# Two score blocks of a map in one accumulator bank, and the summing transfers of a value operand queued earlier

## Chip, cores and metric

One core of one Trainium2 chip. The metric is the device time of one execution in microseconds; the time of a kernel is the median of its timed runs.

## The reference

A decoder trunk of two layers on 512 tokens of width 1024, all in float32. Each layer is a token mixer and a gated feed-forward net, each followed by a residual sum and a layer norm.

```python
for i in range(2):
    h = multiscale_pool(x, ...) if i == 0 else diff_attention(x, ...)
    x = layernorm(ALPHA * x + h)
    x = layernorm(ALPHA * x + (silu(x @ w_gate[i]) * (x @ w_up[i])) @ w_down[i])
```

The change lies at the seam of layer 0's feed-forward net and layer 1's attention, and in the attention:

```python
q, k, v = split(x @ w_qkv, 3)          # 8 heads, 2 maps (c = 0, 1) of 64 columns each; v: 128 columns a head
for qb in range(4):                    # blocks of 128 queries
    s = q[c, block qb] @ k[c, : (qb + 1) * 128].T / 8       # causal: 128, 256, 384, 512 keys
    p = softmax(s + bias)              # bias by distance
    a = p[0] - lam * p[1]
    out = a @ v
```

## The kernel before, in words

**Precision.** A product of two float32 matrices is made as three products of parts: each operand is a rounded high part and the rest, a low part, and high x high, high x low and low x high are summed in an accumulator bank. ACT casts the high part, DVE subtracts it for the low part (`split`, L123 and L124).

**Banks.** There are eight accumulator banks of 128 x 512 float32. `bank(name)` (L62) takes the next one of a pool of eight; a product into it waits until the last reader of the name that had the bank earlier is done.

**Order.** The order on every engine is written out by hand: the code is the schedule, and each engine, and each queue of transfers, takes its instructions in program order. SP issues plain loads, POOL issues transfers that add into their destination ("accumulating" ones), and POOL also makes the small power operation of each layer norm (`spread_of`, L199).

**The end of layer 0's feed-forward net** (`ffn`). The down product is made by a seven-product scheme (Strassen's, in Winograd's form) in the order `DOWN = P1, Q5, P6, Q3, P7, P2, Q4`; each product runs over six pairs of rows of the hidden matrix (`PAIRS`). In the last one, Q4, the two output halves of the first 256 tokens are normed while the products run, and its last three pairs are run once per token block (`tail = 3`). After it the attention begins.

**The value product** of the attention uses the same seven-product scheme, `values(p, r, accs, w)` (L1078 for its products). Three of its weight operands are sums of rows of the weight array `wall`, and these sums are made by transfers:

- `tall`: rows `two_rows(0)`, loaded by SP, then `two_rows(1)` and `two_rows(2)` added by POOL (`tall_step`, L270 to L275). It is cut into parts `vt0`, `vt1` (`wide6`), the operand of product P6. Then `two_rows(3)` is added (L1298), cut into `vu0`, `vu1` (`wide4`), the operand of Q4.
- `short`, in a tile named `vals`: `two_rows(1)` loaded by SP, then `two_rows(2)` added by POOL (L1018, L1019); cut into `vs0`, `vs1` (`wide7`), the operand of P7.

P6, P7 and Q4 all gather in the two banks `va`; between them ACT copies `va` out. Head 0's query and key products stand between P2 and P6. Two further rows (`raw`, L113) are also completed by accumulating transfers on POOL, for the later product Q5.

**A head of the attention.** For head h the code issues, on TensorE: the query product (24 matrix products), for h > 1 a small product of head h - 2, the key product (24), ten transposes of head h - 1's map into three banks `at` (L1185), the scores of four query blocks, then head h - 1's value product `mix`. `scores(h, q)` takes two banks, one for each map c, and runs six products of 64 contraction rows: (query high, key high), (query low, key high), (query high, key low), each for c = 1 and c = 0, the two maps lying on rows 64 to 127 and 0 to 63. `softmax` (L1155 on DVE, L1160 on ACT) reads the banks. The three `at` banks are read by an ACT cast to `ah` and a DVE subtraction to `al`; a bank is free again after the second.

Of the kernel before, what the change touches and what calls it, by code (L numbers as in the profile page):

```python
# [18 lines left out]
P = 128  # L19
S = 512  # L20
# [7 lines left out]
HD = 64  # L28
# [26 lines left out]
def trunk(ctx, tc, x, wall, pscale, lam_p, subln, table, lng, lnb, band, first, onehot, out):  # L55
    nc = tc.nc
# [5 lines left out]
    def bank(name):  # L62
        return ps.tile([P, 512], F32, tag="bank", name=name)
# [206 lines left out]
    def tall_step(step):  # L270
        if step == 0:
            talls.append(keep.tile([P, 2, D], F32, tag="gb", name="tall"))
            nc.sync.dma_start(out=talls[0], in_=two_rows(0))
        else:
            nc.gpsimd.dma_start(out=talls[0], in_=two_rows(step), accum_op=ALU.add)  # L275
# [226 lines left out]
    def ffn(layer, late):  # L502
        n = 2 * layer + 1
        final = n == 2 * DEPTH - 1
# [3 lines left out]
        with tc.tile_pool(name=f"ffn{layer}", bufs=1) as fp:  # L508
# [58 lines left out]
            for k in range(HALF):  # L567
                j0 = index[k] = len(chunks)
                c = c0 + 4 * k
# [16 lines left out]
            for kind, j in steps:  # L586
                c, pair = chunks[j]
# [200 lines left out]
            accs = [(bank(f"g{layer}_{f}"), bank(f"u{layer}_{f}")) for f in range(early)]  # L788
# [104 lines left out]
            f = early  # L893
# [41 lines left out]
            done = store if final else None  # L935
            for p in DOWN:
                j0 = DOWN.index(p) * len(PAIRS)
                if p == "P2" and not final:
                    tall_step(0)
                if p in ("P1", "Q5", "P2"):  # L940
                    banks[p] = [bank(f"{p}_{layer}_{s}") for s in range(2)]
                accs = banks[{"P1": "P1", "Q5": "Q5", "Q3": "Q5", "P2": "P2"}.get(p, "P1")]
                together = len(PAIRS) - (tail if p == "Q4" else 0)
                for i in range(together):
                    j = j0 + i
                    prepare(j + 5, j + 4)
                    if p == "Q4":
                        if i == together - 1:
                            prepare(len(items), len(items))
                            ready(c1 + FB + 2)  # L950
                        for s in range(2):
                            if i == s:
                                spread_of(n, s)
                            if i == s + 1:
                                norm(n, s)
                    if (p, i) == ("Q4", 2) and not final:
                        tall_step(1)
                    multiply(j, accs, range(2))
                for s in range(2):
                    if p == "P1":  # L960
                        add_to(s, 0, accs[s], ALPHA)
                    elif p == "Q5":
                        add_to(2 + s, 1, accs[s], ALPHA)
                    elif p == "P6":
                        add_to(s, 1, accs[s], ALPHA, op=ALU.subtract)
                    elif p == "Q3":
                        add_to(s, 1, accs[s])
                        stat(n, s, 1)
                    elif p == "P7":
                        add_to(2 + s, 1, accs[s], op=ALU.subtract)  # L970
                        stat(n, 2 + s, 1)
                    elif p == "P2":
                        add_to(s, 0, accs[s])
                        stat(n, s, 0)
                    elif p == "Q4":
                        if s == 0 and not final:
                            turn(n, 0)
                        for i in range(len(PAIRS) - tail, len(PAIRS)):
                            if final and s == 0:
                                prepare(j0 + i + 5, j0 + i + 5)  # L980
                                if i == 1:
                                    spread_of(n, 0)
                                    spread_of(n, 1)
                                if i == 2:
                                    norm(n, 0, done)
                            multiply(j0 + i, accs, (s,))
                        add_to(2 + s, 0, accs[s], ALPHA)
                        stat(n, 2 + s, 0)
                        spread_of(n, 2 + s)
                        if final and s == 0:  # L990
                            norm(n, 1, done)
                        norm(n, 2 + s, done)
                        if not final:
                            if s == 0:
                                turn(n, 1)
                            ready(c1 + FB + 3 + s)
            if not final:
                tall_step(2)
            base[0] = c1 + FB


    def attention():
        n = 2
        with tc.tile_pool(name="attn", bufs=1) as ap:
            lp = ap.tile([P, 4, HD], F32, tag="bias", name="lp", bufs=2)
            nc.sync.dma_start(
                out=lp.rearrange("p a b -> p (a b)"),
# [125 lines left out]
                w1 = ap.tile([P, 4], F32, tag="w1", name=f"w1_{h}", bufs=2)  # L1133
                mid[h] = (mn, sm, w1)

            def scores(h, q):
                (qh, ql), (kh, kl) = qk[h, "q"], qk[h, "k"]
                wide = max((q + 1) * P, 256)
                accs = [bank(f"s{h}_{q}_{c}") for c in range(2)]
                qs = slice(q * P, (q + 1) * P)  # L1140
                for i, (a, b) in enumerate(((qh, kh), (ql, kh), (qh, kl))):
                    for c in (1, 0):
                        r = slice(c * HD, (c + 1) * HD)
                        nc.tensor.matmul(  # L1144
                            accs[c][:, :wide], a[r, qs], b[r, :wide], start=i == 0, stop=i == 2
                        )
                maps[h, q] = accs

            def softmax(h, q):
                mn, sm, _ = mid[h]  # L1150
                w = (q + 1) * P
                accs = maps.pop((h, q))
                for c in range(2):
                    p = soft[h][c][:, OFF[q] : OFF[q] + w]
                    nc.vector.tensor_tensor_reduce(  # L1155
                        out=p, in0=accs[c][:, :w], in1=biases[h][:, w - 1 :: -1] if w < S else biases[h][:, ::-1],
                        op0=ALU.add, op1=ALU.min, scale=1.0, scalar=3.0e38,
                        accum_out=mn[:, q, c : c + 1],
                    )
                    nc.scalar.activation(  # L1160
                        p, p, AF.Exp, bias=mn[:, q, c : c + 1], scale=-1.0,
                        accum_out=sm[:, q, c : c + 1],
                    )
# [107 lines left out]
            w = take(2)  # L1271
# [7 lines left out]
            w = take(2)  # L1279
# [55 lines left out]
            for h in range(HEADS):  # L1335
                if h > 0:
                    combine(h - 1, 3)
                if h > 0:
                    split_values(h - 1)
                if h == 0:  # L1340
                    scalars()
                if 1 < h <= SB + 1:
                    affine(n - 1, h - 2)
                if h == SB + 2:
                    load_gb(n)
                if h + 1 < HEADS:
                    load_bias(h + 1)
                if h > 0:
                    accs = [bank(f"{nm}{h}") for nm in "qk"]
                    w = take(2)  # L1350
                    ready(where[0] + {1: 3, last: 3}.get(h, 1))
                    query(accs[0], w[0])
                    split_query(h, "q", accs[0])
                    if h > 1:
                        root(h - 2)
                    query(accs[1], w[1])
                    ready(where[0] + {1: 4, last: 3}.get(h, 2))
                    if h > 1:
                        scaled(h - 2)
                    split_query(h, "k", accs[1])  # L1360
                    if h == 1:
                        w = take(2)
                        for r in range(2):
                            values("Q3", r, vc, w[r])
                        for s in range(2):
                            combined(part(0, 1, s), vc[s], part(0, 1, s), ALU.subtract)
                    transposed(h - 1)
                start_scores(h)
                for q in range(2):
                    scores(h, q)  # L1370
                    softmax(h, q)
                if h == 0:
                    for s in range(2):
                        combined(part(1, 1, s), vc[s], part(1, 1, s), ALU.subtract)
                for q in (2, 3):
                    scores(h, q)
                if h > 0:
                    mix(h - 1)
                if h == last:
                    ready(where[0] + 4)  # L1380
                for q in (2, 3):
                    combine(h, q - 2)
                    softmax(h, q)
                combine(h, 2)
# [144 lines left out]
```

## Time and profile before

| | us |
|---|---|
| median of 3 runs (lowest, highest) | 952.35 (951.37, 953.99) |
| the profiled execution's own time | 954.01 |
| its span, first to last instruction | 952.2 |
| TensorE busy | 933.8 (98%) |
| VectorE (DVE) busy | 788.1 (83%) |
| ScalarE (ACT) busy | 514.4 (54%) |
| GpSimd (POOL) busy | 126.5 (13%) |
| mean granted TensorE clock | 0.993 |

PE is TensorE's matrix products, PEld its weight loads. All positions are microseconds from the start of the span. In a row of the timeline stand the start, the duration, the engine, the line of the code, the operation, `output<-inputs`, the shapes and the number of instructions merged; in square brackets the idle time of the engine ahead of it and what ended it. Records of successive matrix products overlap, so the distance between two starts says what one costs, not its duration.

### The profile page before, as it was taken

Reading aid. Unit: us, or ns where it says so; the run is one execution under the profiler, and the core shown is the slowest. Engines: PE = TensorE matmul, PEld = TensorE weight load, DVE = VectorE, ACT = ScalarE, POOL = GpSimd, SP = SyncE. Lnnn points to the kernel's source line nnn. Section 1 sums busy time; section 2 is a strip of 40 time slices with the busy share of each in tenths; the row PEclk is TensorE's granted clock in tenths of the full one; section 3 lists DMA queues with packets and bytes.
Section 4 is the critical chain, followed back from the end, with each engine's and each line's share of the span. In section 5 each row is a group of like instructions: output and inputs, shape, how many; then the busy total and the mean of one; then the engine's idle time right before and its main releaser. Section 6 shows DMA issues by size and latency. Waiting matters only on the chain.

```text
span 952.2 us, 14942 instructions
## 1 busy us (share of the span) xinstructions
PE 933.8 (98%) x5712; PEld 832.4 (87%) x5712; DVE 788.1 (83%) x1158; ACT 514.4 (54%) x819; POOL 126.5 (13%) x152
## 2 busy tenths in 40 slices
PE   9999999999999999899999999999999999999996
PEld 8898899999988888688888878998899999988884
DVE  7859879999988778767888777779779999987778
ACT  6652444554564457466877853833344554564450
POOL 4121121110001102100211100211111110001101
PEclk9999999999999999999999999999999999999998
DMA  8287988986868977966576532396888886888942
GB/s 242 114 259 240 345 272 246 263 261 206 257 207 284 359 253 181 236 182 167 134 149 161 128 102 91 101 315 215 258 273 245 256 269 205 258 248 278 366 153 89
DMA packets 86039, 211.11 MB, mean 222 GB/s; under 512 B 15141, under 2 KB 26661, under 8 KB 85967
## 3 DMA queue, kind: packets, MB, share of 16 engines
q1 hardware_dynamic: 43420, 117.16, 37.4%
q0 software_dynamic: 18768, 58.20, 24.8%
q10 hardware_dynamic: 23778, 34.78, 10.2%
q8 instruction: 45, 0.74, 0.3%
q14 instruction: 28, 0.22, 0.1%
HBM read 173.40 MB, written 36.72 MB: 221 GB/s over the span
## 4 chain that ended last, share of the span: by engine, by line
PE 89%; DVE 5%; DMA 2%; ACT 2%; issue 1%; POOL 0%; DVEq 0%; SPq 0%; POOLq 0%; ACTq 0%
PE A L859 17%; PE P L926 14%; PE C L859 8%; PE Q L926 6%; PE B L859 4%; PE g L151 3%; PE u L151 3%; PE u L149 3%; PE u L150 3%; PE g L149 3%; PE g L150 3%; PE s L1144 2%; PE va L1078 2%; DMA tall<-in_wall 2%; PE q L149 1%; PE q L151 1%
## 5 line engine op out<-in xcount | busy, mean ns | idle before, releaser
L605 DVE TENSOR_TENSOR raw<-raw,raw 128x1024 f32<-128x1024 f32 x56 | 68.3, 1219 | 0.5
L123 ACT CAST xs<-hid 128x512 fp32r<-128x512 f32 (+1 forms) x60 | 34.7, 582 | 24.4 <-DVE hid L773 24.4
L124 DVE TENSOR_TENSOR xs<-hid,xs 128x512 fp32r<-128x512 f32 (+1 forms) x60 | 38.4, 642 | 7.8 <-ACT xs L123 7.8
L1160 ACT ACTIVATE p<-p,mn 128x128 f32<-128x128 f32 (+3 forms) x64 | 35.2, 552 | 16.0 <-DVE mn L1155 16.0
L249 ACT ACTIVATE y<-pt,bT,gT 128x128 f32<-128x128 f32 x80 | 30.0, 455 | 19.4 <-PE pt L235 19.4
L704 POOL DMA_DIRECT2D b<-in_wall x20 | 14.0, 705 | 174.6 <-DMA tsum<-b 82.2
L765 POOL DMA_DIRECT2D xs<-ssum x24 | 17.4, 725 | 141.5 <-PE Q L926 68.4
L199 POOL TENSOR_TENSOR rs<-rs,mhalf 128x1 f32<-128x1 f32 x16 | 12.6, 792 | 163.0 <-DVE rs L198 123.6
L637 DVE TENSOR_TENSOR hid<-sg,u 128x512 f32<-128x512 f32 x16 | 11.0, 686 | 27.2 <-PE u L151 16.5
L704 POOL DMA_DIRECT2D hid<-in_wall x24 | 18.7, 824 | 79.0 <-DMA tsum<-hid 41.3
L1155 DVE CUSTOM_DVE_ANT_0 p<-s,bias 128x128 f32<-128x128 f32 (+3 forms) x64 | 28.1, 485 | 0.7 <-PE s L1144 0.7
L741 ACT CAST v<-u 128x512 fp32r<-128x512 f32 x22 | 13.6, 620 | 27.3 <-DVE u L739 27.2
L124 DVE TENSOR_TENSOR xt<-y,xt 128x512 fp32r<-128x512 f32 x20 | 13.6, 690 | 13.5 <-ACT xt L123 13.4
L190 DVE BATCH_NORM_STATS2 st<-res 128x6 f32<-128x512 f32 x32 | 22.2, 695 | 1.1
L885 ACT ACTIVATE sg<-sg 128x512 f32<-128x512 f32 x14 | 8.9, 632 | 25.7 <-DVE sg L878 25.7
L705 POOL DMA_DIRECT2D hid<-in_wall x12 | 14.8, 1233 | 56.3 <-DMA hid<-in_wall 49.6
L653 ACT CAST xs<-hid 128x1024 fp32r<-128x1024 f32 x8 | 8.4, 1051 | 23.8 <-DVE hid L670 11.6
L1144 PE MATMUL s<-heads 64*128 64x256 f32 (+2 forms) x168 | 19.9, 353 | 0.0
L874 DVE TENSOR_TENSOR hid<-C,hid 128x512 f32<-128x512 f32 x14 | 9.7, 691 | 10.8 <-PE C L859 9.3
L1174 DVE SCALAR_TENSOR_TENSOR p<-p,sm,p 128x128 f32<-128x128 f32 (+3 forms) x32 | 17.7, 552 | 1.1
L870 ACT COPY hid<-C 128x512 f32<-128x512 f32 x14 | 8.2, 587 | 18.5 <-PE C L859 18.5
L124 POOL TENSOR_TENSOR sql<-sq,sqh 128x512 fp32r<-128x512 f32 x7 | 9.0, 1293 | 65.0 <-ACT sqh L123 65.0
(1187 smaller groups left out, 3678.1 us busy)
## 6 DMA issues: line engine op xcount, KB each, us to landing
raw<-in_wall SPq DMA_DIRECT2D x122, 512.0 KB, 4.9
r<-tsum SPq DMA_DIRECT2D x40, 512.0 KB, 4.5
hid<-in_wall POOLq DMA_DIRECT2D x36, 512.0 KB, 7.2
b<-in_wall POOLq DMA_DIRECT2D x30, 512.0 KB, 5.7
r<-in_wall SPq DMA_DIRECT2D x30, 512.0 KB, 4.7
tsum<-hid ACTq DMA_DIRECT2D x24, 512.0 KB, 6.0
ssum<-v ACTq DMA_DIRECT2D x22, 512.0 KB, 4.0
tsum<-b ACTq DMA_DIRECT2D x20, 512.0 KB, 4.9
```

The source lines that it names most:

```text
L123: nc.scalar.copy(dst_h, src)
L124: (low or nc.vector).tensor_tensor(dst_l, src, dst_h.bitcast(F32), op=ALU.subtract)
L149: nc.tensor.matmul(acc, ah, bh, start=start, stop=False)
L150: nc.tensor.matmul(acc, ah, bl, start=False, stop=False)
L151: nc.tensor.matmul(acc, al, bh, start=False, stop=stop)
L249: nc.scalar.activation(y[:, k, :], pt[:, k * P : (k + 1) * P], AF.Identity, bias=bT[:, n, kk : kk + 1], scale=gT[:, n, kk : kk + 1],)
L605: tt(t, raws[pair[0]], raws[pair[1]], op=ALU.add)
L704: nc.gpsimd.dma_start(out=t[:, j], in_=src[:, j])
L859: nc.tensor.matmul(o, w[:, c], x[:, kk, :], start=p in ("P1", "Q5", "P2") and f + kk + e == 0, stop=p in ("Q4", "Q3", "P2") and (f, kk, e) ...
L926: nc.tensor.matmul(accs[s], x[:, k, r], y[:, c], start=first and k == 0 and e == 0, stop=last and k == m - 1 and e == 2, skip_group_check= ...
L1144: nc.tensor.matmul(accs[c][:, :wide], a[r, qs], b[r, :wide], start=i == 0, stop=i == 2)
L1160: nc.scalar.activation(p, p, AF.Exp, bias=mn[:, q, c : c + 1], scale=-1.0, accum_out=sm[:, q, c : c + 1],)
```

## The change

Two edits.

1. The second and third transfer into `tall` are queued earlier: `two_rows(1)` at the start of Q4 in place of Q4's third pair, `two_rows(2)` at Q4's third pair in place of the end of the net. The first stays at the start of P2.
2. `scores` takes several query blocks. Blocks 0 and 1 are made by one call: for each map c one bank holds block 0 in columns 0 to 255 and block 1 in columns 256 to 511. The order of the twelve products is: both blocks' (query high, key high), both blocks' (query low, key high), both blocks' (query high, key low); within a block c = 0 comes ahead of c = 1, for blocks 2 and 3 too. A head takes six banks for its scores where it took eight.

```diff
             for p in DOWN:
                 j0 = DOWN.index(p) * len(PAIRS)
-                if p == "P2" and not final:
-                    tall_step(0)
+                if p in ("P2", "Q4") and not final:
+                    tall_step(0 if p == "P2" else 1)
...
                     if (p, i) == ("Q4", 2) and not final:
-                        tall_step(1)
+                        tall_step(2)
                     multiply(j, accs, range(2))
...
-            if not final:
-                tall_step(2)
             base[0] = c1 + FB
...
-            def scores(h, q):
+            def scores(h, *qs):
                 (qh, ql), (kh, kl) = qk[h, "q"], qk[h, "k"]
-                wide = max((q + 1) * P, 256)
-                accs = [bank(f"s{h}_{q}_{c}") for c in range(2)]
-                qs = slice(q * P, (q + 1) * P)
+                accs = [bank(f"s{h}_{qs[0]}_{c}") for c in range(2)]
+                outs = {}
+                for n, q in enumerate(qs):
+                    wide = max((q + 1) * P, 256)
+                    outs[q] = [acc[:, 256 * n : 256 * n + wide] for acc in accs]
                 for i, (a, b) in enumerate(((qh, kh), (ql, kh), (qh, kl))):
-                    for c in (1, 0):
-                        r = slice(c * HD, (c + 1) * HD)
-                        nc.tensor.matmul(
-                            accs[c][:, :wide], a[r, qs], b[r, :wide], start=i == 0, stop=i == 2
-                        )
-                maps[h, q] = accs
+                    for q in qs:
+                        for c in range(2):
+                            r = slice(c * HD, (c + 1) * HD)
+                            nc.tensor.matmul(
+                                outs[q][c], a[r, q * P : (q + 1) * P],
+                                b[r, : outs[q][c].shape[-1]],
+                                start=i == 0 and q == qs[0], stop=i == 2 and q == qs[-1],
+                                skip_group_check=True,
+                            )
+                for q in qs:
+                    maps[h, q] = [o[:, : (q + 1) * P] for o in outs[q]]
...
-                        out=p, in0=accs[c][:, :w], in1=...,
+                        out=p, in0=accs[c], in1=...,
...
                 start_scores(h)
+                scores(h, 0, 1)
                 for q in range(2):
-                    scores(h, q)
                     softmax(h, q)
```

More of the change, by code (lines that the diff above doesn't have):

```diff
@@ L1155, in softmax @@
                     nc.vector.tensor_tensor_reduce(
-                        out=p, in0=accs[c][:, :w], in1=biases[h][:, w - 1 :: -1] if w < S else biases[h][:, ::-1],
+                        out=p, in0=accs[c], in1=biases[h][:, w - 1 :: -1] if w < S else biases[h][:, ::-1],
                         op0=ALU.add, op1=ALU.min, scale=1.0, scalar=3.0e38,
```

## The prediction

> **What bounds the kernel now.** I read the page first, then the waits, the chain, the timelines of POOL, ACT and DVE around the seam, and the busy times by stretch.
>
> ```profile
> PE 933.8 (98%) x5712; PEld 832.4 (87%) x5712; DVE 788.1 (83%) x1158; ACT 514.4 (54%) x819; POOL 126.5 (13%) x152
> PE va L1078 <- DVE vals L1261: 4.1, 1, 4.1
> ```
>
> TensorE is busy for 98% of the span, so only its waits and its slow places are worth anything. The second row, the longest of TensorE's waits, lies where the change acts: product P6 of the value operand.
>
> ```profile
> 381.22 0.59 POOL raw L113
> 381.81 16.26 DMA tall<-in_wall
> 398.10 1.05 ACT vt0h L123
> ...
> 400.32 1.22 DVE vt1l L124
> 401.54 0.61 DVE vals L1261
> ...
> 402.29 0.77 PE L1078 MATMUL va<-vt0h,heads 128*128 128x512 f32 x1 [4.13 <-DVE vals L1261]
> 410.56 0.62 PE L1078 MATMUL va<-vs0h,heads 128*128 128x512 f32 x2
> 416.00 0.62 PE L1078 MATMUL va<-vu0h,xt 128*128 128x512 f32 x2
> 398.00:402.00 4.00, 0.15 (x1) 0.00 (x0) 2.82 (x3) 2.48 (x3) 0.16 (x1) 0.79 1.06 256
> 402.00:406.00 4.00, 3.71 (x9) 2.97 (x10) 2.02 (x4) 1.77 (x2) 1.02 (x1) 0.50 0.88 129
> 406.00:410.00 4.00, 4.00 (x17) 3.23 (x16) 3.40 (x4) 1.30 (x3) 0.00 (x0) 0.85 0.96 190
> ```
>
> The chain names the cause: the last addition into `tall` took 381.81 + 16.26 = 398.07 to land, then come the cast, the subtraction, the sum out of bank `va`, and only then P6. The wait costs 4.13 us, and more behind it: P6 runs from 402.29 to P7's start at 410.56, 8.27 us, while P7, the same 24 products, takes 416.00 - 410.56 = 5.44. The stretches say why: after the idle time the granted clock (third number from the end) is 0.50. That is 2.83 us more.
>
> The second place is the scores. Their line alone, by stretch, each from a head's first score product to the next product behind the scores (heads 0, 1 and 2, then the sum over all eight heads):
>
> ```profile
> 426.50:428.65 2.15, 2.13 (x24) 1.72 (x24) 1.00 0.82 200
> 446.29:448.93 2.64, 2.64 (x24) 1.96 (x24) 1.00 1.09 231
> 463.61:466.41 2.80, 2.80 (x24) 2.02 (x24) 1.00 0.95 171
> ...
> sum 21.58, PE 21.55 PEld 15.85; mean PE 2.69 PEld 1.98
> ```
>
> The same 24 products take 2.15 us in head 0 and 2.80 in head 2, at full clock, and TensorE counts as busy throughout, so no table of waits shows it. Head 2 on DVE and TensorE:
>
> ```profile
> 463.24 0.69 DVE L124 TENSOR_TENSOR heads<-k,heads 128x512 fp32r<-128x512 f32 x1 [0.93 <-ACT heads L123]
> 463.85 0.68 DVE L124 TENSOR_TENSOR al<-at,ah 128x512 fp32r<-128x512 f32 x1
> 464.45 0.68 DVE L124 TENSOR_TENSOR al<-at,ah 128x512 fp32r<-128x512 f32 x1
> 465.05 0.41 DVE L124 TENSOR_TENSOR al<-at,ah 128x256 fp32r<-128x256 f32 x1
> 465.38 0.28 DVE L1155 CUSTOM_DVE_ANT_0 p<-s,bias 128x128 f32<-128x128 f32 x1
> 463.61 0.39 PE L1144 MATMUL s<-heads 64*128 64x256 f32 x2
> 463.99 0.50 PE L1144 MATMUL s<-heads 64*128 64x256 f32 x4
> 465.19 0.83 PE L1144 MATMUL s<-heads 64*128 64x512 f32 x3
> 465.52 0.73 PE L1144 MATMUL s<-heads 64*128 64x512 f32 x4
> ```
>
> Two things meet. Block 0's third pair, which reads the keys' low part, starts at 463.99, right after DVE has made it (463.24 + 0.69 = 463.93). And block 3's first product starts at 465.19 alone and the next at 465.52: just after the second and the third `al` subtraction end (465.13 and 465.46). These read the transposes' banks `at`. I infer that block 3's two banks, and one of block 2's (the first `al` ends at 464.53), are those of `at`, so the scores wait for DVE to empty them, and the two maps' products fall out of step.
>
> **Edit 1, the transfers.** No byte is added; two issues move.
>
> ```profile
> 338.64 0.38 SPq L273 DMA_DIRECT2D tall<-in_wall  x1
> DMA to landing us min/median/max: 8.4/12.8/16.3
> 361.62 0.95 POOL L199 TENSOR_TENSOR rs<-rs,mhalf 128x1 f32<-128x1 f32 x1 [37.87 <-DVE rs L198]
> 364.48 1.23 POOL L275 DMA_DIRECT2D tall<-in_wall  x1
> 391.54 1.19 POOL L1019 DMA_DIRECT2D vals<-in_wall  x1 [7.97 <-DMA vals<-in_wall]
> 401.84 1.18 POOL L1298 DMA_DIRECT2D tall<-in_wall  x1 [9.10 <-DVE vt1l L124]
> ```
>
> The first addition now waits on POOL only for the load issued at 338.64. Even at the slowest landing of `tall`'s three additions, 16.3, that load is in by 355, ahead of Q4's first power operation at 361.62, for which POOL has waited 37.87 us, so the POOL work behind it is not held. Issued by 355, it lands by 355 + 12.8 = 368 at the median and at 347 + 12.8 = 360 if the load takes 8.4. The second addition now stands behind Q4's two power operations, where the first one was: 364.48, or 368 if the first is late. It lands at 377 (+12.8), at the latest at 368 + 16.3 = 384. It is no longer behind the `raw` addition of 381.22. What the first addition collides with are SP's loads for Q4's last pairs. Bounded by the spread of landings above, these come 16.3 - 8.4 = 7.9 us later. The cover is that the code prepares four pairs ahead of the products (`prepare(j + 5, j + 4)`); a pair is 12 products, half of P7's 24, so 2.7 us, and four are 10.9. I take 0; without the cover it would be up to 7.9.
>
> What is late next?
>
> ```profile
> 392.92 1.06 ACT L1294 COPY vals<-vb 128x512 f32<-128x512 f32 x2
> 404.23 1.05 ACT L123 CAST vs0h<-vals 128x1024 fp32r<-128x1024 f32 x1 [3.65 <-DMA vals<-in_wall]
> 412.69 1.05 ACT L123 CAST vu0h<-tall 128x1024 fp32r<-128x1024 f32 x1
> ```
>
> - P6: ACT reaches the cast of `vt0` behind the copies, at 392.92 + 1.06 = 393.98 instead of 398.10. P6 starts 402.29 - 398.10 = 4.19 later, at 398.17. TensorE is free at 402.29 - 4.13 = 398.16. The whole wait goes, and with it the half clock.
> - P7 would start at 398.17 + 5.44 = 403.6. `short` must be in by 401.3 (cast and subtraction, 1.05 + 1.23). Now it lands at 404.23; its issue at 391.54 stood behind `tall`'s transfer in POOL's queue until 398.07, so its own bytes took 6.2. Without that: 391.54 + 1.2 + 6.2 = 399; unchanged: 404.2. I take 399.
> - Q4 would start at 409.0. The last addition to `tall` is issued when `vt1` is made, at 401.84 - 4.1 = 397.7; it is behind `short` again, and now ends at 401.84 + 8.4 = 410.2, 6.0 after it. So 399 + 6 = 405 against a need of 409.05 + 0.23 - 2.3 = 407. Unchanged, 410.2, it is 3.3 late.
>
> So edit 1 gives 4.13 + 2.83 = 6.96 us; bounds 6.96 - 3.3 - 2.83 (a second idle stretch at half clock) = 0.8 and 6.96.
>
> By the Trainium skill, "TensorE: Matmul & The Clock Gate", section "What's actually happening", an idle window of about 3.4 us puts the array on half clock. The trace agrees: 4.13 us idle, granted 0.50. By that rule a rest of 3.3 us would be at the edge of paying again.
>
> **Edit 2, the scores.** No product is added or taken away. The low keys' first use moves from the third pair to the fifth. Head 0 and the start of head 2's block 2:
>
> ```profile
> 427.22 0.28 PE L1144 MATMUL s<-krso,qsqh 64*128 64x256 f32 x2
> 427.34 0.34 PE L1144 MATMUL s<-ksq,qsqh 64*128 64x384 f32 x1
> ...
> 464.57 0.50 PE L1144 MATMUL s<-heads 64*128 64x384 f32 x3
> 441.79 0.69 DVE L124 TENSOR_TENSOR heads<-k,heads 128x512 fp32r<-128x512 f32 x1 [1.67 <-ACT heads L123]
> ```
>
> A pair of the two maps' products costs 427.34 - 427.22 = 0.12 there. The low keys are now needed four pairs, at least 0.48, after the first product; they come 0.32 after it (463.93 - 463.61). That wait goes. Two banks fewer a head shift the rotation by two names: blocks 2 and 3 take the banks of older readers, at most one of `at`, emptied at 464.53, 0.92 after the start, when block 3 begins at 6 x 0.12 + 3 x 0.18 = 1.26 (a pair's 0.12, by its width). So I expect every head at head 0's 2.15: 21.58 - 8 x 2.15 = 4.38 us. Bounds: nothing, 0, and 4.38.
>
> What may become late: block 0's softmax must now wait for the whole shared bank, 12 products instead of 6. In head 2 DVE comes to it at 465.38, 1.77 after the first product; the twelve are done after about 0.72 + 0.28 = 1.0, so free. In head 0 DVE does wait, about 0.5 longer, and has 1.67 idle later, at 441.79. A head's period shrinks by 0.65 for DVE:
>
> ```profile
> 498.16 0.69 DVE L124 TENSOR_TENSOR heads<-k,heads 128x512 fp32r<-128x512 f32 x1 [0.85 <-ACT heads L123]
> ```
>
> DVE waits 0.85 a head for the keys, more than 0.65, so it still keeps up; only just.
>
> A page speaks of just such banks: the Trainium skill, "PSUM — Partial Sum Buffer", section "PSUM bank collisions raise a hardware error", says that products of two different row tiles may not write one bank at the same time. Here each shared bank belongs to one map, one row half, so by that rule nothing new collides; no run here shows it yet.
>
> **Sum.** 6.96 + 4.38 = 11.34. Against the profiled execution's 954.01: 942.7; against the median of the runs, 952.35: 941.0. TensorE is bound from there to the end, and the later loads are tied to buffers that it frees, so nothing gives it back.
>
> **The rivals.**
> - *DVE becomes the bound in the heads.* For: 0.85 idle is little above 0.65, and head 0's softmax starts later. Against: DVE's idle time is TensorE's doing. Then edit 2 gives between 0 and 4.38: 941.0 to 945.4.
> - *The next transfer is late.* `vu` lands as late as now: 3.3 lost, 944.3; with half clock again, 947.1. For: POOL's queue is full there. Against: one megabyte less in it.
> - *Slower: the shared bank takes the maps' products out of step.* Place: the 12 products a head of blocks 0 and 1. Now they take 0.96 in head 2 (463.61 to 464.57), 0.08 each. If each waited for the product ahead to be done, 0.28 (the row at 427.22), a head loses 12 x 0.20 = 2.4, eight heads 19.2: 941.0 + 19.2 = 960.2. It decides from 11.34 / 96 = 0.12 us a product on. Against: each bank has one writer at a time, and the net's banks A, B and C hold two column halves in the same way, of which the list of waits names none.
> - *Nothing happens*: POOL is held by something else, and the banks are not the cause: 952.35.
>
> **How the numbers follow.** Forecast 0.72; DVE 0.10; late transfer 0.10; out of step 0.05; nothing 0.03. The runs of this kernel spread over 0.28%, so 0.3% (2.9 us) is about what a measurement can tell from no change. Faster by more: 0.72 + 0.10 + 0.10 = 0.92; within: 0.03; slower: 0.05. The forecast's own range is 941.0 with 1.7 either way (1.3, half the runs' spread, and 0.05 a head for reading the stretches); with the DVE case it holds 0.82: 939.3 to 945.4.
>
> **What would show it.** Right: no wait of `va` on L1261, P6 taking 5.44, the clock at 1.00 there; the additions to `tall` issued near 347 and 364; scores at 2.15 in every head. Wrong: a new wait of `va` at `vs0h` or `vu0h`; DVE without idle time ahead of `heads<-k` and TensorE waiting on it at `at` or `s`; scores longer than 2.8.

## The result and the profile after

| | before | after |
|---|---|---|
| median of 4 runs each (lowest, highest), us | 952.75 (951.37, 953.99) | 942.77 (942.32, 943.55) |
| profiled execution's own time | 954.01 | 942.9 |
| its span | 952.2 | 941.1 |
| mean granted TensorE clock | 0.993 | 0.997 |

The ratio is 0.9897, 95% interval 0.9879 to 0.9914: 10.0 us less. The forecast was 941.0, range 939.3 to 945.4, 92% for faster.

The page and the list of TensorE's waits of the changed kernel, the rows that answer to the first two of the prediction:

```profile
PE 926.7 (98%) x5712; PEld 828.5 (88%) x5712; DVE 786.9 (84%) x1158; ACT 514.2 (55%) x819; POOL 126.7 (13%) x152
PE va L1076 <- DVE vals L1266: 0.2, 1, 0.2
```

The share of TensorE is 98% as before. The wait of 4.1 us is down to 0.2. The seam on TensorE (first the last product of head 0's key, then the first products of P6, P7 and Q4), and the clock in the stretches behind it:

```profile
397.34 0.39 PE L151 MATMUL k<-xt,w73l 128*128 128x512 f32 x1
397.94 0.47 PE L1076 MATMUL va<-vt0h,heads 128*128 128x512 f32 x1 [0.21 <-DVE vals L1266]
403.50 0.39 PE L1076 MATMUL va<-vs0h,heads 128*128 128x512 f32 x1
408.94 0.39 PE L1076 MATMUL va<-vu0h,xt 128*128 128x512 f32 x1
398.00:402.00 4.00, 4.00 (x18) 3.29 (x19) 2.35 (x4) 2.44 (x3) 0.68 (x1) 1.00 0.79 112
402.00:406.00 4.00, 4.00 (x20) 3.30 (x18) 3.47 (x4) 2.92 (x5) 0.00 (x0) 1.00 0.86 170
```

P6 starts 0.60 after the last key product, of which 0.23 is that product itself, and takes 5.56 us; the clock stays at 1.00 where it was 0.50. POOL and ACT of the changed kernel show why:

```profile
344.97 1.23 POOL L275 DMA_DIRECT2D tall<-in_wall  x1 [21.62 <-DMA r<-tsum]
361.21 0.95 POOL L199 TENSOR_TENSOR rs<-rs,mhalf 128x1 f32<-128x1 f32 x1 [15.02 <-DVE rs L198]
364.07 1.21 POOL L275 DMA_DIRECT2D tall<-in_wall  x1
390.49 1.21 POOL L1017 DMA_DIRECT2D vals<-in_wall  x1 [8.69 <-DMA vals<-in_wall]
397.49 1.19 POOL L1303 DMA_DIRECT2D tall<-in_wall  x1 [5.79 <-DVE vt1l L124]
393.74 1.06 ACT L123 CAST vt0h<-tall 128x1024 fp32r<-128x1024 f32 x1
399.56 1.05 ACT L123 CAST vs0h<-vals 128x1024 fp32r<-128x1024 f32 x1 [3.31 <-DMA vals<-in_wall]
406.08 1.05 ACT L123 CAST vu0h<-tall 128x1024 fp32r<-128x1024 f32 x1
```

The two additions go out at 345 and 364. (The first row names `r<-tsum` as what ended POOL's wait; by the transfers' landings it was as forecast the load of `tall`, whose last part landed at 344.39, while that `r` was in only at 345.64.) The cast of `vt0` at 393.74 waits for no transfer any more, `short` is in at 399.56 instead of 404.23, and `vu0` is cast at 406.08 without a wait. The scores' line by head (heads 0, 1, 2, and the sum over eight):

```profile
419.92:422.05 2.13, 2.13 (x24) 1.71 (x24) 1.00 0.89 197
439.70:441.84 2.14, 2.13 (x24) 1.74 (x24) 1.00 1.06 241
456.51:458.65 2.14, 2.14 (x24) 1.74 (x24) 1.00 0.83 155
...
sum 17.09, PE 17.07 PEld 13.86; mean PE 2.13 PEld 1.73
```

Every head takes what head 0 took: 17.09 in all where it was 21.58. In head 2 block 3's first products no longer follow the third subtraction out of the `at` banks:

```profile
457.95 0.41 DVE L124 TENSOR_TENSOR al<-at,ah 128x256 fp32r<-128x256 f32 x1
458.09 0.63 PE L1145 MATMUL s<-heads 64*128 64x512 f32 x4
```

Block 3's products start, in pairs, at 458.09, while that subtraction runs until 457.95 + 0.41 = 458.36; in the kernel before, the second of them started 0.06 after its end.

**Where the span's 11.1 us came from**, by places on TensorE: 0.4 lies ahead of the change (SP's issue of `tall` at 338.2 for 338.64) and isn't its work; from there to Q5's first product 6.2, which is the whole difference of the seam, so the loads that the earlier addition might have delayed cost nothing that shows there; to head 7's transposes 3.8 (heads 1 to 6); from there to the end 0.7 (head 7).

### The profile page after: what moved, and what is told of

The parts are those of the page before. It is cut to its first block, busy times and chain, and to the rows that moved or that the text cites. A ratio compares the mean times of both kernels' runs of the same rounds, so it can differ in the third digit from the quotient of the medians.

```text
span 941.1 us, 14941 instructions
## 1 busy us (share of the span) xinstructions
PE 926.7 (98%) x5712; PEld 828.5 (88%) x5712; DVE 786.9 (84%) x1158; ACT 514.2 (55%) x819; POOL 126.7 (13%) x152
## 4 chain that ended last, share of the span: by engine, by line
PE 89%; DVE 6%; ACT 3%; issue 1%; POOL 0%; DVEq 0%; ACTq 0%; POOLq 0%
PE A L859 17%; PE P L926 14%; PE C L859 9%; PE Q L926 6%; PE B L859 4%; PE g L151 3%; PE u L151 3%; PE u L149 3%; PE u L150 3%; PE g L149 3%; PE g L150 3%; PE s L1145 2%; PE va L1076 2%; PE q L149 1%; PE q L151 1%; PE k L149 1%
## 5 line engine op out<-in xcount | busy, mean ns | idle before, releaser
L704 POOL DMA_DIRECT2D b<-in_wall x20 | 14.0, 706 | 173.6 <-DMA tsum<-b 49.6
L705 POOL DMA_DIRECT2D b<-in_wall x10 | 12.3, 1230 | 38.1 <-DMA b<-in_wall 38.1
```

Source lines behind the costliest of these rows:

```text
L704: nc.gpsimd.dma_start(out=t[:, j], in_=src[:, j])
```

## The experiments

The theory: the seam gains because the second addition no longer stands in POOL's queue behind the additions to `raw`; the scores gain because blocks 2 and 3 no longer wait for the banks of the transposes, and, a smaller and separate thing, because the low keys are needed later. The rivals are in the expectations. The table has the time, the sum of the scores' stretches over eight heads, and the seam: TensorE's idle time ahead of P6, P6's duration, and the way from the last key product's start to Q5's first product. The kernel before was run beside each group, and took 952.72 to 954.16; where that matters, a time is given both against the changed kernel's median and by how far each is under the kernel before beside it.

| kernel | median us | kernel before beside it | scores, sum | idle | P6 | seam |
|---|---|---|---|---|---|---|
| before | 952.75 | | 21.6 | 4.30 | 7.82 | 23.23 |
| after | 942.77 | 952.75 | 17.1 | 0.37 | 5.56 | 17.04 |
| transfers only | 946.25 | 952.72 | 21.6 | 0.00 | 5.53 | 16.64 |
| scores only | 949.20 | 952.72 | 17.1 | 5.24 | 7.11 | 23.46 |
| shared, block by block | 943.04 | 952.72 | 17.9 | 0.06 | 5.54 | 16.71 |
| own banks, high first | 946.60 | 952.72 | 21.8 | 0.00 | 5.54 | 16.65 |
| wait filled | 951.10 | 954.16 | 21.6 | 0.34 | 5.56 | 17.01 |
| first early, second late | 947.65 | 954.16 | 17.1 | 4.14 | 7.18 | 22.43 |
| both at third pair | 949.55 | 954.16 | 17.1 | 0.00 | 5.44 | 16.55 |
| after, again | 942.71 | 953.33 | 17.1 | 0.01 | 5.56 | 16.68 |
| sum ahead of cut | 942.18 | 953.33 | 17.1 | 0.00 | 5.44 | 16.63 |
| map order back | 942.46 | 953.33 | 17.0 | 0.00 | 5.54 | 16.65 |
| second ahead of raw | 944.67 | 953.60 | 17.1 | 0.27 | 6.79 | 18.58 |

(In "wait filled" the last key product comes 4 us later because of the added ones, so its seam is no gain by itself. P6 is taken from its first product to P7's first; in "second ahead of raw" its 6.79 holds a wait of P7.)

### Edit 1 alone, edit 2 alone

```diff
+                if p in ("P2", "Q4") and not final:
+                    tall_step(0 if p == "P2" else 1)   # and step 2 at Q4's third pair; scores as before
```

> Edit 1 alone: the two additions into tall are queued earlier, the scores are as before. If the seam is worth what the two traces show there (from the last key product's start to Q5's first product 23.23 us before, 17.04 after), this kernel is 6.2 us under the kernel before, about 946.6, with P6 starting within 0.6 us of the last key product at full clock and the scores still at 2.64 to 2.80 a head. Rival: the gain needs both edits (head 0's earlier start only lets the scores wait longer); then it is under 6 us and the scores lengthen.

Measured: 946.25, 6.5 us under the kernel before (ratio 0.9933, 0.9920 to 0.9947). The scores stay at 21.6. The transfers give their 6.2 to 6.6 us by themselves (the two seams, 23.23 - 17.04 and 23.23 - 16.64); the rival falls.

```diff
+                scores(h, 0, 1)    # and the new scores(); tall_step(1), tall_step(2) where they were
```

> Edit 2 alone: blocks 0 and 1 share banks, the additions into tall are as before. If the scores' gain is their own (8 x 2.70 before, 8 x 2.14 after: 4.49 us), this kernel is 4.5 us under the kernel before, about 948.3, with 2.14 a head and the wait of P6 unchanged near 4.3 with the clock at half behind it. Rival: DVE's slack is used up, so that part comes back as waits at the transposes or the key split; then it is under 3.5 us.

Measured: 949.20, 3.5 us under (0.9959, 0.9947 to 0.9972, that is 2.7 to 5.0 us). Its trace has the whole gain of the scores, 17.1, and the wait ahead of P6, in this execution longer than before:

```profile
PE va L1078 <- DVE vals L1268: 5.1, 1, 5.1
```

The interval holds the expected 4.5 and the rival's "under 3.5" alike, so the medians do not decide; the traces do. From Q5's first product to the end of the span the kernel before takes 952.2 - 421.0 = 531.2 us and this one 947.2 - 420.7 = 526.5: 4.7 less, as in the changed kernel (941.1 - 414.4 = 526.7). So nothing of the scores' gain came back behind them, and the rival falls. The two edits alone add up to 6.5 + 3.5 = 10.0, the gain of both; that it agrees to a tenth is chance, as each has an interval of more than 1 us either way.

### Order and sharing, apart

```diff
-                for i, (a, b) in enumerate(((qh, kh), (ql, kh), (qh, kl))):
-                    for q in qs:
+                for q in qs:
+                    for i, (a, b) in enumerate(((qh, kh), (ql, kh), (qh, kl))):
```

> The changed kernel with only the order of the twelve products put back: block 0's three pairs, then block 1's, still in shared banks. If the wait for the low keys and the bank waits are two separate things, only the wait for the low keys returns: 0.16 us in heads 2 to 7, about 1 us over the changed kernel, scores at 2.30. Rival one: the order is what made the gain; then the scores are at 2.6 to 2.8 and the kernel is 3.5 to 4.5 us over the changed one. Rival two: only the banks count: no difference.

The scores by head (heads 0, 1, 2, sum):

```profile
419.74:421.87 2.13, 2.13 (x24) 1.72 (x24) 1.00 0.92 161
439.53:441.67 2.14, 2.14 (x24) 1.74 (x24) 1.00 1.06 228
456.34:458.61 2.27, 2.27 (x24) 1.78 (x24) 1.00 1.07 199
...
sum 17.94, PE 17.93 PEld 14.12; mean PE 2.24 PEld 1.77
```

Sharing alone, with the old order, keeps most of the gain: 0.13 to 0.17 a head comes back in heads 2 to 7, and nothing in head 1, where another product stands between the key's cut and the scores. That is 0.85 us in the trace, as the theory had it. The median, 943.04, is 0.3 over the changed kernel, too little to be told by times (its runs reach from 942.65 to 943.36).

```diff
-                accs = [bank(f"s{h}_{qs[0]}_{c}") for c in range(2)]
-                    outs[q] = [acc[:, 256 * n : 256 * n + wide] for acc in accs]
+                    outs[q] = [bank(f"s{h}_{q}_{c}")[:, :wide] for c in range(2)]
...
-                                start=i == 0 and q == qs[0], stop=i == 2 and q == qs[-1],
+                                start=i == 0, stop=i == 2,
```

> The changed kernel with only the sharing put back: four banks for blocks 0 and 1, but the new order, high parts of the keys first. If blocks 2 and 3 wait for the banks of the transposes, whose last subtraction ends 1.85 us after the first score product, that end pins the scores whatever is won ahead of it: 2.64 in head 1 and 2.80 in heads 2 to 7 as before, 4.4 us over the changed kernel. The order alone would then be worth nothing. Rival: the order is worth its 0.16 a head, scores at 2.64; then it is 3.5 over the changed kernel.

```profile
419.16:421.50 2.34, 2.34 (x24) 1.87 (x24) 1.00 0.73 151
439.14:441.77 2.63, 2.63 (x24) 1.95 (x24) 1.00 1.06 223
456.45:459.25 2.80, 2.80 (x24) 2.02 (x24) 1.00 0.98 192
...
sum 21.75, PE 21.74 PEld 15.91; mean PE 2.72 PEld 1.99
```

With a bank of their own for each block, the new order is worth nothing: 2.80 in heads 2 to 7 as in the kernel before, 946.60, 3.8 us over the changed kernel. What is won at the low keys is waited for at the banks, whose release is tied to DVE's last subtraction. So the bank is the cause and the order is worth something only once the bank wait is gone. In head 2 block 3's first two products start at 458.03 and 458.36, each 0.06 after the end of one of DVE's last two subtractions out of `at`, as in the kernel before. (Head 0, which has no transposes ahead of it, takes 0.21 longer here than in any other kernel. There block 3's second product starts at 420.61, 0.06 after DVE's second read of block 0 has ended, 420.26 + 0.29 = 420.55. In the new order block 0 is done, and so read, later, and I infer that block 3 takes its banks: the same wait for another reader.)

### The clock behind the wait

```diff
+            for k in range(6):            # 18 of the key's 24 products, once more
+                mm3(wide(accs[1], 0, S), tuple(t[:, k * P : (k + 1) * P] for t in w[1]), x_at(k, 0, S), k == 0, k == 5)
             query(accs[1], w[1])
```

> The kernel before, with TensorE kept busy in its wait ahead of P6: the first 18 of the 24 products of head 0's key are run twice (18 x 0.227 = 4.1 us of the 4.3 that it idles). Nothing else changes. If the slow P6 (7.82 us where P7 takes 5.44) comes from the clock that falls in the idle time, P6 runs at clock 1.00 in 5.44 and the kernel is 2.4 us under the one before, about 950.3, though it does more work. Rival: P6 is slow because its operands arrive slowly; then P6 stays near 7.8 and the time at 952.7.

P6's and P7's first products, and the stretch of P6:

```profile
402.50 0.47 PE L1078 MATMUL va<-vt0h,heads 128*128 128x512 f32 x1 [0.18 <-DVE vals L1261]
408.06 0.39 PE L1078 MATMUL va<-vs0h,heads 128*128 128x512 f32 x1
402.00:406.00 4.00, 3.82 (x17) 2.93 (x16) 2.09 (x4) 1.62 (x2) 1.18 (x1) 1.00 0.81 129
```

P6 starts when it did, at 402.5, but at clock 1.00, and takes 5.56 for 7.82. The kernel does 4.1 us more work and is 3.1 us faster (0.9970, 0.9959 to 0.9982, that is 1.7 to 3.9 us); the two traces account for about 2 of it: P6 is shorter by 2.26 and starts 0.21 later. The slow P6 was the clock, not its operands.

### Where the second addition stands in POOL's queue

```diff
-                    if (p, i) == ("Q4", 2) and not final:
-                        tall_step(2)                      # back to the end of the net; step 1 stays early
```

> The changed kernel with only the second addition put back to the end of the net. If what counts is that this addition stands in POOL's queue behind the addition to raw at 380.7, it is issued at about 381 and lands at 395 to 398 again: the wait of P6 and the half clock are back, 4 to 6.2 us over the changed kernel, 947 to 949. Rival: the first addition's earlier landing frees the transfer engines, the second lands by 393 and the kernel stays at 943.

```profile
380.66 1.55 POOL L275 DMA_DIRECT2D tall<-in_wall  x1
401.02 0.47 PE L1076 MATMUL va<-vt0h,heads 128*128 128x512 f32 x1 [3.99 <-DVE vals L1266]
408.20 0.39 PE L1076 MATMUL va<-vs0h,heads 128*128 128x512 f32 x1
400.00:404.00 4.00, 2.98 (x8) 2.41 (x9) 3.20 (x5) 2.21 (x3) 1.18 (x1) 0.69 0.43 51
```

The addition goes out at 380.66 as in the kernel before, the wait is back with the half clock behind it (0.69 is the mean of that stretch: the clock fell to 0.50 at 401.51, when P6 had just begun), and the time is 947.65. That is 4.9 over the changed kernel's median, and 6.5 under the kernel before beside it where the changed kernel was 10.0 under, so 3.5 over by that reckoning; the seam is 22.43 - 17.04 = 5.4 longer. With the first addition early and the second late the idle time is 4.14; the two traces with both late have 4.30 and 5.24. So the early first addition alone hardly moves this wait.

```diff
-                if p in ("P2", "Q4") and not final:
-                    tall_step(0 if p == "P2" else 1)
+                if p == "P2" and not final:
+                    tall_step(0)
...
                     if (p, i) == ("Q4", 2) and not final:
+                        tall_step(1)
                         tall_step(2)
```

> The changed kernel with the first addition left at Q4's third pair, as in the kernel before, and the second right behind it. The second must wait on POOL until the first has landed (364.1 + about 12 = 376), and the power operation of the next token block, which POOL did at 372.5, stands behind it. If POOL's order is a real price, that operation comes near 378, the norm and the transposes behind it 5 us late, TensorE idles about 5 us there and pays half clock once: 5 to 8 us over the changed kernel, 948 to 951, while P6 itself no longer waits for tall. Rival: the power operation has slack; then the kernel is within 1 us of the changed one and the early start of the first addition was not needed.

POOL, the wait that appears, and the clock behind it:

```profile
377.12 1.20 POOL L275 DMA_DIRECT2D tall<-in_wall  x1 [11.77 <-DMA tall<-in_wall]
377.89 1.02 POOL L199 TENSOR_TENSOR rs<-rs,mhalf 128x1 f32<-128x1 f32 x1
PE pt L235 <- DVE res L208: 6.0, 1, 6.0
376.00:380.00 4.00, 0.18 (x1) 0.18 (x2) 1.05 (x2) 0.10 (x1) 2.77 (x3) 0.88 0.27 30
380.00:384.00 4.00, 4.00 (x14) 3.52 (x15) 3.76 (x7) 2.99 (x8) 0.00 (x0) 0.50 1.03 202
```

The second addition waits on POOL for the first to land; the norm's power operation behind it comes at 377.89, TensorE idles 6.0 us at the transposes that need that norm and then runs at 0.50. 949.55 is 6.8 over the changed kernel's median; against the kernel before beside it, it is 4.6 under in place of 10.0, so 5.4 over. P6 waits for nothing. So both moves belong together: the first makes room for the second to be issued without holding POOL.

```diff
-                    if (p, i) == ("Q4", 2) and not final:
-                        tall_step(2)
...
                             if s == 0:
                                 turn(n, 1)
+                            else:
+                                tall_step(2)              # ahead of the second addition to raw
                             ready(c1 + FB + 3 + s)
```

> The changed kernel with the second addition put between Q4's last power operation and the second addition to raw: POOL reaches it at about 379, some 15 us later than in the changed kernel and 2 us earlier than in the kernel before. With a landing of 12.8 to 16.3 us it is in at 392 to 395, and P6 would wait between nothing and 1.5 us, too short for the clock to fall if the fall needs the 4 us that it had in the other traces: 0 to 1.5 us over the changed kernel, P6 in 5.5. Rival: any wait drops the clock; then P6 takes about 7 and the kernel is 2 to 3 us over the changed one.

```profile
401.25 1.05 ACT L123 CAST vs0h<-vals 128x1024 fp32r<-128x1024 f32 x1 [5.48 <-DMA vals<-in_wall]
PE va L1076 <- ACT vals L1313: 1.1, 1, 1.1
402.00:406.00 4.00, 2.93 (x14) 2.09 (x13) 3.66 (x4) 3.65 (x6) 0.00 (x0) 1.00 0.77 153
```

`tall` is in, at 393.26, by the time that ACT comes to its cast (393.29, without a wait), and P6 idles only 0.27, as in the changed kernel (0.37) for DVE's sum out of `va`. But now `short` is late: it is cast at 401.25, ACT's copy of `va` stands behind its casts, and P7 waits 1.1 us for that copy. The time, 944.67, is 1.9 over the changed kernel's median, or 8.9 under the kernel before beside it in place of 10.0, so 1.1 over; the seam is 1.5 longer. The size is near what was expected, but it comes by another wait. The clock stays at 1.00 through this wait: the rival that any wait drops it falls.

### Two small variations

> The changed kernel once more, as the measure for the two beside it: 942.8, 9.9 us under the kernel before.

> The changed kernel with DVE's sum out of the banks va (which P6 overwrites) put ahead of the cut of vt0 and vt1. In the changed kernel P6 still starts 0.37 us late because that sum ends at 397.7, behind the two subtractions. DVE idles 0.69 before the first of them, so the sum costs it about 0.6 there and P6 waits only for the first subtraction, at about 396.4: P6 follows the key product at once and the kernel gains 0.4 us, about 942.4. Rival: the second cut comes 0.6 later and P6's second half waits for it; no gain.

```diff
+            for s in range(2):
+                combined(part(0, 0, s), va[s], part(0, 0, s), ALU.add)
             wide6 = [pair_of(f"vt{r}", tall[:, r]) for r in range(2)]
             nc.gpsimd.dma_start(out=tall, in_=two_rows(3), accum_op=ALU.add)
-            for s in range(2):
-                combined(part(0, 0, s), va[s], part(0, 0, s), ALU.add)
```

Measured: 942.71 (942.28 to 943.44) for the changed kernel again, 942.18 (941.83 to 942.73) with the sum moved. P6 follows at once and takes 5.44 for 5.56, but the changed kernel's second profile idles only 0.01 there, so the 0.37 of the first was of that one execution and there was 0.1 to win. The lowest time of all, and not told apart from the changed kernel.

> The changed kernel with the maps' order put back, c = 1 ahead of c = 0. The order of the maps is a part of the change that I priced at nothing: scores at 2.14 in every head and the time within 0.5 us of the changed kernel. Rival: the order decides which of two banks is waited for first; then the scores lengthen by 0.1 to 0.6 a head, 1 to 4.5 us.

```diff
-                        for c in range(2):
+                        for c in (1, 0):
```

Measured: 942.46, scores at 2.13 in every head. That is 0.25 under the changed kernel beside it, too little to be told: the order of the maps is worth nothing that shows.

## Why the prediction was right, point by point

- *Edit 1.* The wait, the clock and the issue times came as forecast (347 and 364 forecast, 345 and 364 seen; `short` 399 and 399.56). The first addition came 2 us ahead of the earliest forecast because its load took 344.39 - 338.23 = 6.2 us; the prediction had bounded a plain load by the landings of additions, 8.4 at the least. Nothing hung on it. Two sizes were off, and in opposite directions. The half clock was priced at 2.83 from merged rows, whose start is not that of P7's first product. These rows of the kernel before are:

```profile
397.76 0.39 PE L151 MATMUL k<-xt,w73l 128*128 128x512 f32 x1
410.11 0.39 PE L1078 MATMUL va<-vs0h,heads 128*128 128x512 f32 x1
415.55 0.39 PE L1078 MATMUL va<-vu0h,xt 128*128 128x512 f32 x1
```

  P6 took 410.11 - 402.29 = 7.82, so the clock cost 7.82 - 5.44 = 2.38. The idle time was 402.29 - 397.76 - 0.23 = 4.30, not 4.13. Together 6.68 for 6.96, of which the changed kernel's profile gave back 0.49 (0.37 idle, P6 0.12 longer) and its second profile 0.13. Nor is 2.38 a fixed price: in two other traces the clock behind this wait cost 1.67 and 1.74 (last section).
- *Edit 2.* 4.38 forecast, 21.58 - 17.09 = 4.49 seen. The inference that block 3 and half of block 2 take the `at` banks also follows from the code: with banks given out in turn, the eighth name after the first `at` bank is block 2's second bank, and the next two are block 3's. The two experiments that part sharing from order bear it out. Block 3 begins 458.09 - 456.51 = 1.58 after the first product, where the prediction reckoned 1.26; both are later than the 0.92 at which the one `at` bank still in use comes free.
- *DVE "only just" keeps up* was a wrong reading. Its idle time before `heads<-k` is the same in the changed kernel; head 3 in the kernel before, then in the changed one:

```profile
480.72 0.69 DVE L124 TENSOR_TENSOR heads<-k,heads 128x512 fp32r<-128x512 f32 x1 [0.87 <-ACT heads L123]
472.95 0.69 DVE L124 TENSOR_TENSOR heads<-k,heads 128x512 fp32r<-128x512 f32 x1 [0.87 <-ACT heads L123]
```

  That time is the way from TensorE's key product over ACT's cast to DVE, and it moves along with the product. It is not the slack that a shorter head uses up; how much slack DVE has was not measured, only that the change did not use it up (edit 2 alone).
- *The next transfer is late*: it was not, but the run with the second addition ahead of `raw` showed the mechanism, and that my limit for `short` left out ACT's copy of `va` behind the casts. In that run P7 could have followed at 397.48 + 5.44 = 402.92, so by the prediction's working (2.3 for cast and subtraction) `short` was needed by 400.6. Cast at 401.25 it was 0.6 late by that, but P7 started at 404.27, 1.35 late.
- *From the sum to the time.* 11.34 was taken from the median, 941.0. The sum belongs to the profiled execution, 954.01, which lay 1.3 above the median of the four runs (1.7 above that of the three that the prediction had); against it the forecast was 942.7, and the profiled execution after took 942.9. That accounts for most of the 1.8 by which the median was missed. That 942.7 and 942.9 are so close is partly luck: the sum was 0.7 too large (11.34 for the 6.19 and 4.49 that the traces show), and 0.4 of the difference lies ahead of the change.

On the two places of the Trainium skill: "TensorE: Matmul & The Clock Gate" has the half clock after an idle window of about 3.4 us. The runs agree so far that the clock fell to 0.50 at waits of 4.0 to 6.0 us and stayed at 1.00 at the wait of 1.1. But counted from the end of the last product (397.76 + 0.39 = 398.15) it fell after 2.2 us in the kernel before, at 400.35, and after 4.5 and 5.0 in two other runs, so 3.4 us of idle time is not by itself the limit here. What the prediction said of a rest of 3.3 us no run tests. "PSUM — Partial Sum Buffer" forbids two row tiles in one bank at the same time; each shared bank has one row half, and its products ran in step.

## What to carry to other kernels

A unit that counts as busy can still wait: compare the same group of instructions from stage to stage, and when one stage takes longer, set the starts of its instructions beside the ends of the readers of whatever buffer they may have inherited. Of a moved transfer, price the place in the issuing engine's queue on both sides, what it stood behind and what now stands behind it; here one move without the other cost 3.5 to 4.9, or 5.4 to 6.8 us. And take a difference worked out from a profile off that profile's own time, and take starts from rows of a single instruction, not from merged ones.

## What the runs showed of the hardware that was not expected

The price of an idle stretch is not a function of its length alone: after waits of 4.30, 5.24 and 4.14 us the 24 products of P6 took 7.82, 7.11 and 7.18 us, against 5.44 at full clock. The traces show what it hung on. These are the whole stretches of half clock in the kernel before, with the scores alone, and with the second addition late (after the comma TensorE's busy time, its products in brackets; the granted clock is the third number from the end):

```profile
400.35:407.17 6.82, 4.88 (x12) 3.85 (x13) 4.84 (x7) 2.71 (x4) 1.18 (x1) 0.50 0.97 169
402.62:406.04 3.42, 3.36 (x8) 2.72 (x9) 1.48 (x3) 1.44 (x2) 0.79 (x1) 0.50 0.58 99
401.51:404.92 3.41, 3.41 (x9) 2.66 (x9) 2.61 (x3) 2.48 (x3) 0.24 (x1) 0.50 0.74 106
```

The half clock lasted 3.4 us in two of them and twice that in the first (6.83 also in the run with both additions at the third pair, from 379.05 to 385.88). Inside, P6's products start 0.43 us apart; right behind, 0.23. So about half of TensorE's busy time inside is lost, 2.44, 1.68 and 1.71 us, and P6 was longer by 2.38, 1.67 and 1.74. The wait of 4.30, neither the longest nor the shortest, had the highest price, because the clock fell earliest in it, at 400.35, and stayed low twice as long; in the third run it fell only when P6 had begun. What sets the moment of the fall is not shown, and each is one execution.

And 4.1 us of useless products in the first of these waits made the kernel 3.1 us faster (951.10 against 954.16).
